# Grouped-query attention: the query norm factor as the exponential's per-row scale, from 16 columns

## The chip, the cores and the metric

The kernel runs on one core of a Trainium2 chip. A core has several engines with queues of their own: TensorE (matmuls; PE in the profile, with its weight loads as PEld), VectorE (DVE), ScalarE (ACT), GpSimd (POOL) and SyncE (SP), which here issues most of the transfers. Each engine takes its instructions in a fixed order. Matmul results go to PSUM, which has eight banks of 128 x 512 fp32 values; everything else lives in SBUF. The metric is the device time of one execution in microseconds, the median of several runs. One execution was also profiled; its rows are what the text quotes.

## The reference

The program is a two-layer encoder over 512 tokens with 1024 features in fp32. Layer 0 mixes neighbourhood attention with a bidirectional state-space scan; layer 1 is grouped-query attention with 16 query heads of 64 features and 4 key/value heads. A gated feed-forward block follows each. The change lies in layer 1:

```python
def odd_mixer(x, mix_norm, w_qkv, q_norm, k_norm, w_out):
    ...
    proj = rms_norm(x, mix_norm) @ w_qkv
    q, k, v = jnp.split(proj, [GQA_Q_WIDTH, GQA_Q_WIDTH + GQA_KV_WIDTH], axis=-1)
    q = rms_norm(q.reshape(Bsz, S, GQA_HEADS, GQA_HEAD_DIM), q_norm)
    k = rms_norm(k.reshape(Bsz, S, GQA_KV_HEADS, GQA_HEAD_DIM), k_norm)
    ...
    q = apply_rope(q, cos, sin)
    k = apply_rope(k, cos, sin)
    return gqa_block_attention(q, k, v) @ w_out
```

`rms_norm` divides a head's 64 features by the root of their mean square (plus 1e-6) and multiplies by a learned gain per feature. So each query of each head has one scalar factor, and the scores of that query, q·k/8, are linear in it. The softmax over the 512 keys follows.

## The kernel before, in words

All activations are kept transposed: features on the 128 partitions, 512 tokens on the free axis. An fp32 product is made of three faster matmuls: each operand is split into a high and a low part (the high part is a rounded copy by ScalarE, the low part a subtraction by VectorE or GpSimd), and low-high, high-low and high-high are summed in PSUM (`mm3`, L165 to L167).

Layer 1 is `odd_mixer`. Its steps, with the names that the rows carry:

- `project` makes the key projection in two banks (`kpa`, `kpb`), and ScalarE and VectorE square it. The sum of squares over the 1024 input features gives two things: `rt`, 4 columns of the input norm factor (tokens on partitions, L1200 to L1205), made by four fp32 matmuls with a slice of `acc` as the stationary operand (`orst`); and `em`, a full 128 x 512 tile of the epsilon term (L1206 to L1209).
- `head_rstd` (L1211) turns squares into a norm factor per head and token, spread over the 32 partitions that belong to the head: one fp32 matmul with the block matrix `bo32` (L1213), a VectorE instruction that adds the epsilon term, then `rsqrt_tile`: logarithm, exponential and square on ScalarE (L214 to L216) and a Newton step of two VectorE instructions (L208, L209). All work on 128 x 512 tiles. It is called once for the keys and once for each of the four query groups.
- `q_blocks(g)` projects one group of four heads in two blocks, each of eight filler steps of three matmuls. Its squares are summed (L1263), and `q_finish` is put off by `OD_AFTER` = 4 steps (`after`, `step`).
- `q_finish(g)` rotates the two halves by the rotary tables (six VectorE instructions, L1171 to L1173), calls `head_rstd`, multiplies both halves by the factor (L1275), splits them (the subtraction is on VectorE for group 0, on GpSimd for the others) and stacks them by 16 transfers into the four `QS` tiles (L1188) that the score matmuls read.
- The sweep (L1410) has 32 steps and three more to drain. Step i issues `scores(i)` for one half of the 512 queries of head i // 2: two tiles of 128 queries by 512 keys. Each takes two matmuls (L1293, L1294) into one of two `s` banks, a row maximum by VectorE (L1296), the exponential with the negative maximum as bias and the row sum as accumulated output by ScalarE (L1298, read out by one more short instruction), a reciprocal by VectorE (L1299) and the scaling by GpSimd (L1300). Step i also transposes the probabilities of step i - 2 (L1309, split at L1312 and L1313) and multiplies those of step i - 3 with the values (L1326, L1327; L1334 to L1337 make the context).
- Between these, `run(fill, n)` takes filler steps from a stream: the projections of groups 1 to 3 (48 steps) and then the blocks of the output projection (two times 32 steps). `OD_FILL` of them come ahead of the sweep and `OD_QUOTA[i]` in step i. An output block waits for the context of its heads with `while ctxb[2 * part + 1] is None: yield`; a step taken while it waits issues nothing.

The order of the instructions on each engine is not quite the program's: in this layer a planner orders them by dependences and its own costs when the program is built, and puts in the waits. In the feed-forward blocks the order of TensorE, VectorE and ScalarE is the written one.

Of the kernel before, what the change touches and what calls it, by code (L numbers as in the profile page):

```python
# [11 lines left out]
AF = mybir.ActivationFunctionType  # L12
ALU = mybir.AluOpType
# [4 lines left out]
P = 128  # L18
S = 512
D = 1024  # L20
KB = D // P
EPS = 1e-6
# [4 lines left out]
HD = 64  # L27
# [14 lines left out]
NSLOT = 12  # L42
NA_QUOTA = (12, 12, 10, 10, 8, 8, 6, 6, 6, 6)
DT_STEP = 96
OD_FILL = 8
OD_AFTER = 4
OD_QUOTA = (5, 5, 4, 2, 2, 2, 2, 2, 2, 8, 2, 2, 2, 2, 0, 0, 3, 2, 5, 0, 3, 6, 1, 0, 2, 1, 1, 3, 1, 1, 6, 2, 2, 2, 2)
LEAD = (15, 12, 14, 8)
SSD_QUOTA = ((10, 9, 10, 0, 12), (10, 8, 10, 5, 12), (11, 8, 10, 0, 15), (10, 8, 10, 1, 12))
NORM_LAG = (12, 14, 10, 8)  # L50
# [27 lines left out]
def encoder_kernel(ctx: ExitStack, tc: tile.TileContext, xt, vec, cst, rope, nab, w_v, w_qk, w_dt, w_ssd,  # L78
                   w_o0, w_t0, w_fa, w_fb, w_kv, w_gv, w_gq, w_o1, out):
    nc = tc.nc  # L80
    V, A, G, T = nc.vector, nc.scalar, nc.gpsimd, nc.tensor
# [13 lines left out]
    def bank(name, tag="p"):  # L95
        if tag in turns:
            turns[tag].append(turns[tag].pop(0))
            tag = turns[tag][-1]
        return pp.tile([P, S], F32, name=name, tag=f"p{tag}", bufs=BANKS[tag])

    def slot(name, dt=F32):
        return sp.tile([P, S], dt, name=name, tag="s")
# [12 lines left out]
    def small(name, cols, bufs=3, parts=P, dt=F32):  # L115
        return sm.tile([parts, cols], dt, name=name, tag=f"sm_{name}", bufs=bufs)
# [9 lines left out]
    def cs(n, w=None):  # L126
        o = COFF[n]
        return cstt[:, o:o + (w or dict(_CST)[n])]
# [42 lines left out]
    def stream(blocks, ahead):  # L171
        ws = []
        for n, (_, matmuls) in enumerate(blocks):
            while len(ws) < min(len(blocks), n + 1 + ahead):
                ws.append(blocks[len(ws)][0]())
            yield from matmuls(ws[n])
# [30 lines left out]
    def newton(r, t, m):  # L207
        V.scalar_tensor_tensor(t, t, -0.5, m, ALU.mult, ALU.mult)  # L208
        V.scalar_tensor_tensor(r, t, 1.5, r, ALU.add, ALU.mult)  # L209

    def rsqrt_tile(m, name):
        r = slot(f"{name}_r")
        t = slot(f"{name}_t")
        A.activation(r, m, AF.Ln)  # L214
        A.activation(r, r, AF.Exp, scale=-0.5)
        A.activation(t, r, AF.Square)  # L216
        newton(r, t, m)
        return r

    def rsqrt_small(m, r, t):  # L220
        A.activation(r, m, AF.Ln)
        A.activation(r, r, AF.Exp, scale=-0.5)
        V.tensor_tensor(t, r, r, ALU.mult)
        newton(r, t, m)
# [926 lines left out]
    def odd_mixer(op):  # L1151
# [15 lines left out]
        def rotate(pa, pb, tabs, name):  # L1167
            outs = []
            for n, (ta, tb, op) in enumerate(((tabs[0], tabs[1], ALU.subtract), (tabs[2], tabs[3], ALU.add))):
                a, b = slot(f"{name}_ra{n}"), slot(f"{name}_rb{n}")  # L1170
                V.tensor_tensor(a, pa, ta, ALU.mult)  # L1171
                V.tensor_tensor(b, pb, tb, ALU.mult)
                V.tensor_tensor(a, a, b, op)  # L1173
                outs.append(a)
            return outs
# [4 lines left out]
        def split(t, name, mk=sslot, eng=V):  # L1180
            hi, lo = mk(f"{name}_sh"), mk(f"{name}_sl")
            A.activation(hi, t, AF.Copy)
            eng.tensor_tensor(lo, t, f(hi), ALU.subtract)
            return hi, lo

        def stack(dst, parts, r):
            for n, src in enumerate(parts):
                nc.sync.dma_start(f(dst)[32 * n:32 * n + 32], f(src)[32 * r:32 * r + 32])  # L1188
# [10 lines left out]
        ra, rb = rotate(pa, pb, ktab, "k")  # L1199
        pst = bank("orst", "c")  # L1200
# [2 lines left out]
        rt, rtm, rtt = small("ort", 4, 1), small("ortm", 4, 1), small("ortt", 4, 1)  # L1203
        V.tensor_scalar(rtm, pst[:, 0:4], 1.0 / D, EPS, ALU.mult, ALU.add)
        rsqrt_small(rtm, rt, rtt)  # L1205
        ss = bank("oss", "c")  # L1206
        T.matmul(ss, ones, acc, start=True, stop=True)
        em = slot("oem")
# [2 lines left out]
        def head_rstd(sq, name):  # L1211
            ps = bank(f"{name}_ss", "s")
            T.matmul(ps, cs("bo32"), sq, start=True, stop=True)  # L1213
            m = slot(f"{name}_m")
            V.scalar_tensor_tensor(m, ps, 1.0 / HD, em, ALU.mult, ALU.add)
            return rsqrt_tile(m, name)

        r = head_rstd(ksq[0], "ok")
# [25 lines left out]
        def step(flush=False):  # L1244
            for item in list(later):
                item[0] -= 1
                if flush or item[0] <= 0:
                    later.remove(item)
                    item[1]()
# [19 lines left out]

        def q_finish(g, banks, sq):  # L1270
            ra, rb = rotate(*banks, qtab, f"q{g}")
            r = head_rstd(sq, f"oq{g}")
            eng = G if g else V
            for t in (ra, rb):
                V.tensor_tensor(t, t, r, ALU.mult)  # L1275
            (ah, al), (bh, bl) = split(ra, f"qa{g}", eng=eng), split(rb, f"qb{g}", eng=eng)
            QS = []
            for j in range(4):
                qs = lane(f"QS{g}_{j}", "qs", 7, F32R)
                stack(qs, (ah, bh, al, bl), j)  # L1280
                QS.append(qs)
            qs_of[g] = QS

        qs_of, pair, probs, trans = {}, {}, {}, {}

        def scores(i):
            h, u = divmod(i, 2)
            g, j = divmod(h, 4)
            QS = qs_of[g]
            pr = []  # L1290
            for t in (2 * u, 2 * u + 1):
                sps = bank(f"os{h}_{t}", "s")
                T.matmul(sps, QS[j][:, t * P:(t + 1) * P], KHL[g][:, 1], start=True, stop=False)  # L1293
                T.matmul(sps, QS[j][:, t * P:(t + 1) * P], KHL[g][:, 0], start=False, stop=True)  # L1294
                mx, sums = small("omx", 1, 6), small("osum", 1, 6)
                V.tensor_reduce(mx, sps, AX.X, ALU.max, negate=True)  # L1296
                p_ = lane(f"op{h}_{t}", "p", PB)
                A.activation(p_, sps, AF.Exp, bias=mx, accum_out=sums)  # L1298
                V.reciprocal(sums, sums)  # L1299
                G.tensor_scalar(p_, p_, sums, 1.0, ALU.mult, ALU.mult)  # L1300
                pr.append(p_)
            probs[i] = pr
# [63 lines left out]
        def run(gen, n=None):  # L1366
            for _ in (gen if n is None else range(n)):
                if n is not None:
                    next(gen, None)
                step()  # L1370
# [13 lines left out]
        for t in range(4):  # L1384
            ps = bank(f"gv{t}", "s")
# [18 lines left out]
        fill = stream(blocks, 2)  # L1404
        run(fill, OD_FILL)
        step(True)
# [3 lines left out]
        for i in range(32 + lag_v):  # L1410
            n = OD_QUOTA[i]
            cuts = (0, (n + 2) // 3, (2 * n + 2) // 3, n)
# [16 lines left out]
    with tc.tile_pool(name="op", bufs=1, reuse_waits="tile") as op:  # L1429
        odd_mixer(op)  # L1430
# [133 lines left out]
```

## Time and profile before

| what | value |
|---|---|
| median of 3 runs | 1268.25 us (1267.84 to 1270.19) |
| profiled execution | 1268.15 us |
| its span, first to last instruction | 1266.3 us |
| granted TensorE clock | 1.000 |
| matmul records | 7574 |
| score tiles: matmul pairs, maxima, exponentials | 64 each |
| query groups through `head_rstd` | 4 |

The profile's page gives for each engine the time in which it was busy; matmuls are pipelined, so a busy TensorE is not always one at its peak. A row of a group of instructions has its line, engine and operation, the tiles out<-in, the shape and count, then the busy time in us, the mean of one in ns, and the idle time of the engine before them with what ended it. A row in order of time has its start and its length in us. A waits row reads: who waited for whom, the total in us, how often, and the longest.

### The profile page before, as it was taken

How to read it: one execution, taken by the hardware profiler on the slowest of the kernel's cores; microseconds unless marked ns; L12 is line 12 of the kernel's file. 1: busy time of each engine (PE TensorE's matmuls, PEld its weight loads, DVE VectorE, ACT ScalarE, POOL GpSimd, SP SyncE). 2: the span in 40 equal slices, each digit the busy share in tenths (PEclk: the TensorE clock that was granted, in tenths of full speed). 3: DMA queues.
4: the chain of work that ended last, by engine and by line, in shares of the span. 5: the costliest groups of instructions: out<-in, count | busy, mean ns of one | idle time of the engine just before them, and what ended most of it. 6: DMA issues, size and time to landing. Idle time of an engine off the chain costs nothing.

```text
span 1266.3 us, 20167 instructions
## 1 busy us (share of the span) xinstructions
PE 1253.5 (99%) x7574; PEld 1098.5 (87%) x7574; DVE 993.4 (78%) x1669; ACT 731.5 (58%) x1384; POOL 119.1 (9%) x161
## 2 busy tenths in 40 slices
PE   9999999999999999999999999999999999999998
PEld 7777788888788999989998888788888999889987
DVE  6788798999779988739954779989779988558732
ACT  6676578778465556515643558787564566326521
POOL 5022110011000000000000014444000000000000
PEclk9999999999999999999999999999999999999999
DMA  6335343546243333323223452320232333323132
GB/s 232 108 108 159 104 150 117 160 142 198 83 149 101 100 109 109 117 84 100 78 80 111 132 126 77 100 51 27 75 121 93 113 107 101 117 83 101 55 119 93
DMA packets 54241, 139.03 MB, mean 110 GB/s; under 512 B 7232, under 2 KB 9664, under 8 KB 54144
## 3 DMA queue, kind: packets, MB, share of 16 engines
q1 hardware_dynamic: 53712, 137.13, 35.1%
q8 instruction: 59, 0.97, 0.3%
q10 hardware_dynamic: 432, 0.63, 0.2%
q14 instruction: 38, 0.31, 0.1%
HBM read 127.11 MB, written 2.23 MB: 102 GB/s over the span
## 4 chain that ended last, share of the span: by engine, by line
PE 94%; DVE 2%; ACT 2%; DMA 1%; issue 0%; DVEq 0%; ACTq 0%
PE fo L165 6%; PE fo L167 6%; PE fo L166 6%; PE fa L167 5%; PE fa L166 5%; PE fa L165 5%; PE fu L1029 3%; PE fg L1029 3%; PE g L165 3%; PE g L166 3%; PE g L167 3%; PE fb L167 3%; PE fb L165 3%; PE fb L166 3%; PE opt L1309 2%; PE vps L286 2%
## 5 line engine op out<-in xcount | busy, mean ns | idle before, releaser
L165 PE MATMUL fo<-hh,wf_l 128*128 128x512 f32 x352 | 137.0, 389 | 0.0
L166 PE MATMUL fo<-hl,wf_h 128*128 128x512 f32 x352 | 137.0, 389 | 0.0
L167 PE MATMUL fo<-hh,wf_h 128*128 128x512 f32 x352 | 136.9, 389 | 0.0
L152 ACT ACTIVATE wf_h<-wf_r 128x1024 fp32r<-128x1024 f32 (+1 forms) x72 | 65.6, 915 | 119.3 <-PE fo L167 67.6
L1002 DVE TENSOR_TENSOR xr<-xr,fo 128x512 f32<-128x512 f32 (+1 forms) x49 | 32.1, 674 | 109.1 <-PE fo L167 109.1
L1300 POOL TENSOR_SCALAR op<-op,osum 128x512 f32<-128x512 f32 x64 | 45.7, 720 | 504.7 <-DMA QS<-qa_sh 433.3
L154 DVE TENSOR_TENSOR wf_l<-wf_r,wf_h 128x1024 fp32r<-128x1024 f32 (+1 forms) x72 | 74.0, 1044 | 11.1 <-ACT wf_h L152 11.1
L166 PEld LDWEIGHTS fo<-hl,wf_h 128*128 128x128 f32 x352 | 66.1, 188 | 13.8
L167 PEld LDWEIGHTS fo<-hh,wf_h 128*128 128x128 f32 x352 | 66.1, 188 | 13.8
L165 PEld LDWEIGHTS fo<-hh,wf_l 128*128 128x128 f32 x352 | 66.1, 188 | 13.5
L165 PE MATMUL g<-n_xh,w_l 128*128 128x512 f32 x192 | 76.9, 401 | 0.8 <-ACT grp L546 0.8
L166 PE MATMUL g<-n_xl,w_h 128*128 128x512 f32 x192 | 75.3, 392 | 0.5 <-DVE n_xl L189 0.5
L167 PE MATMUL g<-n_xh,w_h 128*128 128x512 f32 x192 | 75.3, 392 | 0.0
L926 ACT ACTIVATE sl<-sb 128x256 f32<-128x256 f32 x36 | 15.1, 421 | 96.0 <-DVE sb L925 96.0
L1298 ACT ACTIVATE op<-os,omx 128x512 f32<-128x512 f32 x64 | 43.8, 687 | 17.3 <-DVE omx L1296 16.7
L807 ACT ACTIVATE sa<-fa 128x256 f32<-128x256 f32 x72 | 27.0, 375 | 37.9 <-PE fa L167 37.9
L1313 DVE TENSOR_TENSOR opt<-opt,opt 128x512 fp32r<-128x512 f32 x64 | 43.4, 683 | 4.8 <-ACT opt L1312 4.2
L1312 ACT ACTIVATE opt<-opt 128x512 fp32r<-128x512 f32 x64 | 38.2, 597 | 14.7 <-PE opt L1309 14.2
L1296 DVE TENSOR_REDUCE omx<-os 128x1 f32<-128x512 f32 x64 | 42.3, 680 | 5.0 <-PE os L1294 4.7
L810 DVE TENSOR_TENSOR gl<-gr,gh 128x1024 fp32r<-128x1024 f32 x36 | 43.9, 1218 | 0.0
L165 PEld LDWEIGHTS g<-n_xh,w_l 128*128 128x128 f32 x192 | 36.1, 188 | 8.4 <-ACT grp L546 1.2
L807 ACT ACTIVATE gh<-gr 128x1024 fp32r<-128x1024 f32 x36 | 37.7, 1049 | 9.4 <-PE fo L167 9.4
(2745 smaller groups left out, 4314.8 us busy)
## 6 DMA issues: line engine op xcount, KB each, us to landing
ur<-in_w_fa SPq DMA_DIRECT2D x36, 512.0 KB, 3.6
gr<-in_w_fa SPq DMA_DIRECT2D x36, 512.0 KB, 3.6
w_r<-in_w_ssd SPq DMA_DIRECT2D x24, 512.0 KB, 3.6
wf_r<-in_w_fb SPq DMA_DIRECT2D x32, 320.0 KB, 3.0
wf_r<-in_w_fa SPq DMA_DIRECT2D x16, 512.0 KB, 3.7
wf_r<-in_w_fb SPq DMA_DIRECT2D x16, 512.0 KB, 3.5
nb<-in_nab SPq DMA_DIRECT2D x16, 256.0 KB, 3.1
ec<-ecumd SPq DMA_DIRECT2D x32, 128.0 KB, 2.9
```

The source lines that it names most:

```text
L152: A.activation(hi[:, 0:cols], raw, AF.Copy)
L154: (eng or V).tensor_tensor(lo[:, 0:cols], raw, f(hi)[:, 0:cols], ALU.subtract)
L165: T.matmul(ps, wl[:, a], xh[:, b], start=first, stop=False, skip_group_check=skip)
L166: T.matmul(ps, wh[:, a], xl[:, b], start=False, stop=False, skip_group_check=skip)
L167: T.matmul(ps, wh[:, a], xh[:, b], start=False, stop=last, skip_group_check=skip)
L807: A.activation(dst, src, AF.Copy, scale=scale)
L810: V.tensor_tensor(lo, t, f(hi), ALU.subtract)
L1029: T.matmul(ps, (wl if p == 0 else wh)[:, k * P:k * P + P], xl if p == 1 else xh, start=m == 0, stop=m == 23)
L1296: V.tensor_reduce(mx, sps, AX.X, ALU.max, negate=True)
L1298: A.activation(p_, sps, AF.Exp, bias=mx, accum_out=sums)
L1300: G.tensor_scalar(p_, p_, sums, 1.0, ALU.mult, ALU.mult)
L1313: V.tensor_tensor(hl[:, S:2 * S], pt, f(hl[:, 0:S]), ALU.subtract)
```

## The change

The factor of a query no longer goes into the query. `q_finish` leaves the rotated query as it is and makes the factor as 16 columns, with the tokens on the partitions: for each of the four blocks of 128 tokens one matmul with that slice of the squares as stationary operand and four columns of `bo32` (one per head of the group) as the moving one. The epsilon term comes from `emc`, four columns made beside `rt`, and the root from `rsqrt_small`, which does the same steps on the small tile. The score tile in PSUM is then without its factor; `scores` multiplies the negative row maximum by the factor (128 x 1, VectorE) and gives the factor as the exponential's scale per row. The keys are treated as before. `OD_FILL` and four entries of `OD_QUOTA` change as well.

```diff
-OD_FILL = 8
+OD_FILL = 9
 OD_AFTER = 4
-OD_QUOTA = (5, 5, 4, 2, 2, 2, 2, 2, 2, 8, 2, 2, 2, 2, 0, 0, 3, 2, 5, 0, 3, 6, 1, 0, 2, 1, 1, 3, 1, 1, 6, 2, 2, 2, 2)
+OD_QUOTA = (5, 5, 1, 2, 2, 2, 2, 2, 2, 8, 2, 2, 2, 3, 0, 0, 3, 8, 5, 0, 3, 6, 1, 0, 2, 1, 1, 3, 1, 1, 6, 0, 2, 2, 2)
...
         rsqrt_small(rtm, rt, rtt)
+        emc = small("oemc", 4, 1)
+        V.tensor_scalar(emc, pst[:, 0:4], EPS / D, EPS * EPS, ALU.mult, ALU.add)
...
             ra, rb = rotate(*banks, qtab, f"q{g}")
-            r = head_rstd(sq, f"oq{g}")
+            ps = bank(f"oq{g}_ss", "s")
+            for t in range(4):
+                T.matmul(ps[:, 4 * t:4 * t + 4], sq[:, t * P:(t + 1) * P], cs("bo32")[:, 0:P:32], start=True, stop=True)
+            m, r, tt = (small(f"oq{n}", 16, 2) for n in "mrt")
+            V.scalar_tensor_tensor(m.rearrange("p (t j) -> p t j", t=4), ps[:, 0:16].rearrange("p (t j) -> p t j", t=4),
+                                   1.0 / HD, emc.unsqueeze(2).to_broadcast([P, 4, 4]), ALU.mult, ALU.add)
+            rsqrt_small(m, r, tt)
+            rows[g] = r
             eng = G if g else V
-            for t in (ra, rb):
-                V.tensor_tensor(t, t, r, ALU.mult)
...
                 V.tensor_reduce(mx, sps, AX.X, ALU.max, negate=True)
+                row = rows[g][:, 4 * t + j:4 * t + j + 1]
+                V.tensor_tensor(mx, mx, row, ALU.mult)
                 p_ = lane(f"op{h}_{t}", "p", PB)
-                A.activation(p_, sps, AF.Exp, bias=mx, accum_out=sums)
+                A.activation(p_, sps, AF.Exp, bias=mx, scale=row, accum_out=sums)
```

More of the change, by code (lines that the diff above doesn't have):

```diff
@@ L1282, in q_finish @@
             qs_of[g] = QS
-        qs_of, pair, probs, trans = {}, {}, {}, {}
+        qs_of, rows, pair, probs, trans = {}, {}, {}, {}, {}
         def scores(i):
```

## The prediction

> **What bounds the kernel now.** I read the page first, then the busy time by stretches over the second half, then the waits of TensorE in the stretches where it is not full, then rows in order of time for the price of single instructions.
>
> ```profile
> span 1266.3 us, 20167 instructions
> PE 1253.5 (99%) x7574; PEld 1098.5 (87%) x7574; DVE 993.4 (78%) x1669; ACT 731.5 (58%) x1384; POOL 119.1 (9%) x161
> ```
>
> The profiled execution took 1268.15 us: the span of 1266.3 and 1.85 around it. All sums below start there; the median of the runs, 1268.25, is 0.1 higher. TensorE is busy for 99% of the span, so nothing that VectorE or ScalarE save is worth anything by itself. It counts only where TensorE waits for them, or where TensorE's own work changes. The query norm lies in the grouped-query layer; its sweep over 32 steps of two score tiles (16 heads by two halves) runs from 747.8 to 886.5 us. Stretches of it, with the columns PE, weight loads, DVE, ACT, POOL, granted clock, DMA share and GB/s:
>
> ```profile
> 750.00:800.00 50.00, 49.81 (x281) 42.01 (x280) 45.44 (x88) 36.43 (x77) 18.22 (x23) 1.00 0.42 114
> 800.00:840.00 40.00, 37.71 (x216) 29.78 (x214) 36.57 (x74) 32.01 (x70) 21.56 (x25) 1.00 0.25 60
> 840.00:880.00 40.00, 40.00 (x257) 34.85 (x255) 36.32 (x76) 32.67 (x73) 17.56 (x24) 1.00 0.11 34
> 880.00:905.00 25.00, 24.98 (x143) 20.66 (x142) 17.88 (x31) 13.97 (x28) 4.72 (x6) 1.00 0.15 44
> L1293 PE MATMUL os<-K,QS x64: 387/398/682, 747.8 to 886.5; 128*128 128x512 f32 x64
> ```
>
> TensorE shows 0.19 us of idle time in the first stretch, 2.29 in the second, none in the third. VectorE stands at 91% in all three: here it is nearly a second bound. The waits, TensorE's from 800 to 840 us (five rows), from 750 to 800 (the sixth), and last the weight loads' waits for the exponential from 700 to 910:
>
> ```profile
> PE opt L1309 <- DVE opt L1313: 0.7, 1, 0.7
> PE oq_ss L1213 <- ACT op L1298: 0.5, 1, 0.5
> PE o L165 <- ACT cx_sh L1182: 0.4, 1, 0.4
> PE os L1293 <- ACT op L1298: 0.3, 1, 0.3
> PE oc L1326 <- DVE ocx L1335: 0.2, 1, 0.2
> PE os L1293 <- ACT op L1298: 0.2, 1, 0.2
> PEld os L1293 <- ACT op L1298: 4.6, 12, 0.7
> ```
>
> These 2.3 us are what the sweep loses in plain sight. Some more is hidden: a score matmul's weight load waits 12 times for an exponential to free one of the two score banks, 4.6 us in all, of which 0.5 comes out as idle TensorE.
>
> **TensorE's share of the change.** Per query group, one 512-column fp32 matmul goes, and four come whose stationary operand is a 128x128 slice of the squares and whose moving operand has four columns. Their form stands in the trace at L1202, with one column:
>
> ```profile
> 715.03 0.95 PE L1202 MATMUL orst<-cstt,o_acc 128*128 128x1 f32 x8
> 717.56 1.02 PE L1213 MATMUL ok_ss<-oksq,cstt 128*128 128x512 f32 x2
> ```
>
> Each fp32 matmul leaves two records. Four small ones take 0.95 us, the wide one 1.02. So 4 x (0.95 - 1.02) = -0.3 us; sixteen columns are not a sixteenth of the price. Bounds: 0 to -0.3.
>
> **VectorE and ScalarE in the norm.** Removed per group are five wide VectorE instructions (L1215, L208, L209, twice L1275) and three wide ScalarE ones (L214 to L216). A queue of them runs at this pace:
>
> ```profile
> 820.01 0.68 DVE L1171 TENSOR_TENSOR q_ra<-q,qt_tab 128x512 f32<-128x512 f32 x1
> 820.62 0.68 DVE L1172 TENSOR_TENSOR q_rb<-q,qt_tab 128x512 f32<-128x512 f32 x1
> 821.21 0.68 DVE L1215 SCALAR_TENSOR_TENSOR oq_m<-oq_ss,oem 128x512 f32<-128x512 f32 x1
> 821.81 0.68 DVE L1173 TENSOR_TENSOR q_ra<-q_ra,q_rb 128x512 f32<-128x512 f32 x1
> 821.95 0.62 ACT L214 ACTIVATE oq_r<-oq_m 128x512 f32<-128x512 f32 x1
> 822.60 0.63 ACT L215 ACTIVATE oq_r<-oq_r 128x512 f32<-128x512 f32 x1
> 823.27 0.63 ACT L216 ACTIVATE oq_t<-oq_r 128x512 f32<-128x512 f32 x1
> ```
>
> From start to start that is 0.60 us on VectorE and 0.66 on ScalarE: 3.0 and 2.0 us less per group. Group 0 is finished before the sweep, so within the sweep VectorE loses 9.0 and ScalarE 6.0. What replaces them are four small VectorE and two small ScalarE instructions per group, and 64 multiplications of 128x1, one per score tile, between the row maximum and the exponential. The price of a small instruction depends on its neighbours:
>
> ```profile
> 844.77 0.16 DVE L1299 RECIPROCAL osum<-osum 128x1 f32<-128x1 f32 x1
> 844.85 0.67 DVE L1356 TENSOR_TENSOR xr<-xr,o 128x512 f32<-128x512 f32 x1
> 720.69 0.16 DVE L223 TENSOR_TENSOR ortt<-ort 128x4 f32<-128x4 f32 x1 [1.01 <-ACT ort L222]
> 720.77 0.69 DVE L1381 TENSOR_TENSOR wgvl<-wgv_r,wgvh 128x512 fp32r<-128x512 f32 x1
> 721.37 0.15 DVE L208 SCALAR_TENSOR_TENSOR ortt<-ortt,ortm 128x4 f32<-128x4 f32 x1
> 721.45 0.68 DVE L1209 TENSOR_SCALAR oem<-oss 128x512 f32<-128x512 f32 x1
> 722.04 0.15 DVE L209 SCALAR_TENSOR_TENSOR ort<-ortt,ort 128x4 f32<-128x4 f32 x1
> 30.57 0.16 DVE L223 TENSOR_TENSOR rtt<-rt 128x4 f32<-128x4 f32 x1
> 30.76 0.16 DVE L208 SCALAR_TENSOR_TENSOR rtt<-rtt,rtm 128x4 f32<-128x4 f32 x1
> ```
>
> With another wide instruction behind it, a small one moves the queue on by 0.08 us (844.77 to 844.85), though it lasts 0.16. Directly behind the instruction that it depends on it costs 0.20 (30.57 to 30.76). Bounds of one multiplication are thus 0.08 and 0.20. I take 0.08, because in the same layer (720.69 to 722.04) the planner put a wide instruction between each pair of a dependent chain. The 64 then cost 5.1 us (12.8 at the other end), the three groups' small ones 12 x 0.08 = 1.0 (2.4). VectorE's balance over the sweep is -9.0 + 5.1 + 1.0 = -2.9 us, or +6.2 at the other end.
>
> The duration alone speaks against the change: 0.16 us for one column against 0.68 for 512. [...]
>
> The exponential gets a second per-row operand. The trace has one activation with both from PSUM, against today's exponential:
>
> ```profile
> L530 ACT ACTIVATE grp<-g,vect 128x512 f32<-128x512 f32 x16 | 12.4, 775 | 19.3 <-PE g L167 19.3
> L1298 ACT ACTIVATE op<-os,omx 128x512 f32<-128x512 f32 x64 | 43.8, 687 | 17.3 <-DVE omx L1296 16.7
> L222 ACT ACTIVATE ort<-ort 128x4 f32<-128x4 f32 x1 | 0.2, 206 | 0.0
> ```
>
> That is 88 ns more, 5.6 us over 64. With the six small ones at 0.2 each (the last row), 1.2 us, ScalarE's balance in the sweep is -6.0 + 5.6 + 1.2 = +0.8 us: nothing at 73 to 82% busy. The new small term emc (L1206 of the new file) is one more 0.15 us beside 0.68 us instructions, hidden under gv matmuls: nothing.
>
> **What of it reaches TensorE.** First, the burst. After the third group's projection VectorE runs six rotations, then the five norm instructions, between 816 and 829 us, and score tiles queue behind them. The rotations stay, and so do the waits for ocx, cx_sh and the bank of oq_ss (1.1 us of the five rows). The waits that come after (0.7 for the transposed probabilities, 0.3 for the exponential) go with 3.0 us of norm work taken out ahead of them; about half as much again is hidden in slower matmul starts: -1.5. The first two bursts show 0.2 and something hidden: -0.3. Second, the price: every tile's bank is held longer by 0.08 + 0.09 = 0.17 us. On 12 waits this is 2.0 us if all comes out and 0.2 at the share that comes out now (0.5 of 4.6); I take 0.2, since the score matmuls have other matmuls ahead of them.
>
> Third, the filler. Counting the steps that the quotas allow, after stage 2 the new kernel has done 20 where the old one had 22, after stage 12 46 against 48, after stage 13 49 against 50, and from stage 16 both stand at 52. There the next step needs the context of heads 6 and 7, which stage 18 delivers; steps asked for until then yield without a matmul. So the quota of 8 in stage 17 moves nothing, and both reach 53 in stage 18 and leave 28 for the end. The third query group's finish comes one stage (about 4.3 us) later, behind stage 15:
>
> ```profile
> 840.68 0.59 SPq L1188 DMA_DIRECT2D QS<-qb_sl  x1
> 855.08 0.48 PE L1293 MATMUL os<-K,QS 128*128 128x512 f32 x1
> L165 PE MATMUL g<-n_xh,w_l 128*128 128x512 f32 x192 | 76.9, 401 | 0.8 <-ACT grp L546 0.8
> ```
>
> Its last stacking transfer is issued 14.4 us before the first scores of that group, so the delay is covered, and the shorter chain gives some of it back. No transfer is added; the sixteen of a group only come ready sooner. Two filler steps of three matmuls fewer in the early stages cost nothing while TensorE's idle time there is 0.2 us; without cover it is at most 2 x 3 x 0.40 = 2.4.
>
> The sum: -0.3 - 1.5 - 0.3 + 0.2 = -1.9 us, 1268.15 - 1.9 = 1266.3 us. Against the median this is 0.16% less, and about 0.2% (2.5 us) is what a measurement of this kernel tells from no change.
>
> **The rivals.** One: all that waits is relieved. The visible 2.5 us of 750 to 905 go, and half of the 4.6 of the weight loads with them: 1268.15 - 2.5 - 2.3 = 1263.4. For it: VectorE, at 91%, is the one that is late in the burst. Against: three of the five visible waits stand ahead of the removed work. Chance 0.23.
>
> Two, slower: the multiplication stands directly behind its maximum and VectorE becomes the bound after the bursts.
>
> ```profile
> 800.00:840.00 40.00, 11.86 (x18) 1.00 0.25 60
> 840.00:880.00 40.00, 13.31 (x21) 1.00 0.11 34
> ```
>
> These are the row maxima in two stretches. In the second nothing is removed, and 21 multiplications at 0.20 take 4.2 us where VectorE has 3.68 free; in the first 18 x 0.20 = 3.6 eat the 3.0 that the burst saves. With VectorE's free time there mostly forced by its inputs, some 3 of the 4.2 us come out: 1268.15 + 3 = 1271.2. It decides from 3.68 / 21 = 0.175 us per tile on. For it is the pair at 30.57; against, the chain at 720.69. [...] Chance 0.19.
>
> Three, it does nothing: TensorE's work is even, and a new order puts as many waits elsewhere as it removes: 1268.2. For it is that 99% leave little. Chance 0.18.
>
> **How the numbers follow.** The forecast has 0.40, with its own range 1264.8 to 1267.5; about a third of it lies below 1265.7 and counts as faster. Faster is then 0.23 + 0.14 = 0.37, slower 0.19, and the rest, 0.44, is the same. The range reaches from below rival one's 1263.4 to rival two's 1271.2: 1262.4 to 1271.2.
>
> **What would show it.** Right: the small matmuls at about 0.95 us per group; the exponential near 775 ns; TensorE's idle time from 800 to 840 us down from 2.3 to about 1.2, with ocx and cx_sh still in the list; small multiplications with a wide instruction ahead of them; nothing moved before 715 us, and the last feed-forward layer shifted as a whole. Wrong: the weight loads' waits for the exponential well above 4.6 us, or VectorE over 95% from 840 to 880 us; or a saving over 4 us, which the waits named here could not hold without the hidden ones.

## The result, and the profile after

The changed kernel takes 1278.28 us (median of 4 runs, 1277.93 to 1280.85) against 1268.14 us of the kernel before beside it: ratio 1.0086, 95% interval 1.0074 to 1.0098. That is 10.1 us more, where 1.9 us less was forecast, and above the end of the range (1271.2). The profiled execution took 1278.18 us, its span is 1276.2.

The page of the kernel after, first lines:

```profile
span 1276.2 us, 20222 instructions
PE 1262.8 (99%) x7598; PEld 1098.9 (86%) x7598; DVE 996.5 (78%) x1730; ACT 730.0 (57%) x1380; POOL 121.0 (9%) x161
```

TensorE is still "99% busy", and 9.3 us longer so, in a span that is 9.9 us longer: busy time doesn't show the loss. The stretches of the sweep, columns as in the prediction (PE, weight loads, DVE, ACT, POOL, clock, DMA share, GB/s):

```profile
750.00:800.00 50.00, 49.43 (x278) 40.88 (x277) 42.92 (x99) 33.89 (x71) 19.32 (x23) 1.00 0.38 100
800.00:840.00 40.00, 37.37 (x218) 29.49 (x216) 36.85 (x87) 30.20 (x65) 18.51 (x22) 1.00 0.34 91
840.00:880.00 40.00, 39.09 (x230) 31.77 (x229) 36.05 (x87) 31.28 (x67) 16.51 (x22) 1.00 0.13 37
880.00:905.00 25.00, 24.92 (x153) 20.76 (x152) 22.46 (x50) 18.70 (x39) 10.67 (x13) 1.00 0.12 30
```

The counts hint at it: from 840 to 880 us TensorE now runs 230 matmuls where it ran 257. They are no measure, because the windows hold other work: the sweep starts at 749.5 us instead of 747.8, and in another order. Waits of the weight loads and of TensorE from 740 us on, after:

```profile
PEld os L1300 <- ACT op L1307: 9.4, 29, 0.7
PEld oc L1335 <- DVE opt L1322: 4.9, 11, 0.9
...
PE os L1300 <- ACT op L1307: 1.4, 5, 0.4
```

The score matmuls' weight loads wait for an exponential 29 times instead of 12 and twice as long in all (9.4 against 4.6 us). The two new operations themselves, by groups:

```profile
L1307 ACT ACTIVATE op<-os,omx,oqr 128x512 f32<-128x512 f32 x64 | 49.4, 776 | 12.9 <-DVE omx L1305 12.6
L1305 DVE TENSOR_TENSOR omx<-omx,oqr 128x1 f32<-128x1 f32 x64 | 12.8, 204 | 0.1
```

Where the time went, by the starts of the same matmuls in both traces: the first projection starts 0.65 us later (87.02 against 86.37; over all the traces of this study it lies between 85.0 and 87.0); from there to the key projection of layer 1 it takes 619.2 us instead of 617.8 (+1.4), although nothing in this stretch was changed; layer 1, from there to the start of the last feed-forward block, takes 220.5 instead of 213.1 (+7.4); the last block adds 0.4. So there are two losses, one of them outside the edited code.

### The profile page after: what moved, and what is told of

It is laid out like the page before. It is cut to its first block, busy times and chain, and to the rows that moved or that the text cites. A ratio compares the mean times of both kernels' runs of the same rounds, so it can differ in the third digit from the quotient of the medians.

```text
span 1276.2 us, 20222 instructions
## 1 busy us (share of the span) xinstructions
PE 1262.8 (99%) x7598; PEld 1098.9 (86%) x7598; DVE 996.5 (78%) x1730; ACT 730.0 (57%) x1380; POOL 121.0 (9%) x161
## 4 chain that ended last, share of the span: by engine, by line
PE 92%; DVE 4%; ACT 2%; issue 1%; DMA 0%; POOL 0%; DVEq 0%; ACTq 0%; POOLq 0%
PE fo L166 6%; PE fo L167 6%; PE fo L165 6%; PE fa L167 5%; PE fa L165 5%; PE fa L166 5%; PE fu L1029 3%; PE fg L1029 3%; PE g L166 3%; PE g L165 3%; PE g L167 3%; PE fb L165 3%; PE fb L167 3%; PE fb L166 3%; PE vps L286 2%; PE opt L1318 1%
## 5 line engine op out<-in xcount | busy, mean ns | idle before, releaser
L1307 ACT ACTIVATE op<-os,omx,oqr 128x512 f32<-128x512 f32 x64 | 49.4, 776 | 12.9 <-DVE omx L1305 12.6
```

The source lines that it names most:

```text
L1307: A.activation(p_, sps, AF.Exp, bias=mx, scale=row, accum_out=sums)
```

## Experiments

All times are medians. "Above before" is the difference to the kernel before in the same batch, whose median lay between 1267.46 and 1268.28 us. The way of a tile is the time from the start of its maximum to the start of its exponential.

**Parts of the change, left as the planner orders them.** First the multiply is taken off the way to the exponential, left out, or kept without the scale:

```diff
# e1 (e2 has the second pair alone, without the multiply)
-V.tensor_tensor(mx, mx, row, ALU.mult)
+V.tensor_tensor(small("ojk", 1, 6), mx, row, ALU.mult)
-A.activation(p_, sps, AF.Exp, bias=mx, scale=row, accum_out=sums)
+A.activation(p_, sps, AF.Exp, bias=mx, scale=one1, accum_out=sums)
# e3
-V.tensor_tensor(mx, mx, row, ALU.mult)
+V.tensor_tensor(mx, mx, one1, ALU.mult)
-A.activation(p_, sps, AF.Exp, bias=mx, scale=row, accum_out=sums)
+A.activation(p_, sps, AF.Exp, bias=mx, accum_out=sums)
```

> The multiplication of the row maximum is still issued for each of the 64 score tiles, but writes a tile that nothing reads; the exponential takes the plain maximum as bias and a column of ones as scale (the query norm factor is left out of the scores). Chain theory (the multiplication stands one wide VectorE instruction behind its maximum, so that each score bank is held about 0.7 us longer): 1269 to 1272 us, the weight loads' waits for the exponential fall from 9.4 to below 6 us. Occupancy theory (VectorE is full, 64 more instructions are too many): stays at 1277 to 1279. Scale theory (the exponential's second operand, 88 ns a tile): stays at 1277 to 1279. Filler theory: stays.

> The multiplication is not issued at all; the exponential takes the plain maximum as bias and a column of ones as scale (the query norm factor is left out of the scores). Chain theory: like the run with the multiplication off the chain, within 1.5 us (1269 to 1272). Occupancy theory: 1268 to 1271, and clearly below the run that issues it off the chain. Scale theory and filler theory: 1276 to 1279.

> The multiplication stays in the chain, with a column of ones in place of the factor, and the exponential has no scale operand (the query norm factor is left out). Chain theory and occupancy theory: 1275 to 1278, at most 2 us less than the changed kernel. Scale theory: 1269 to 1272; the exponential back at about 687 ns in either case.

Measured: e1, off the way, 1279.69 us (ratio 1.0091, 1.0076 to 1.0106); e2, without the multiply, 1273.97 (1.0046, 1.0032 to 1.0061); e3, without the scale, 1280.82 (1.0098, 1.0083 to 1.0113). Taking the multiply out of the way gains nothing, taking it out altogether gains 4.3 us, and the scale is not the cause (in e3 too the norm factor stays out of the scores). Without the multiply 5.8 us of the loss are still there.

All three times lie outside the ranges of every theory, e1's by 0.7 us, and e1 speaks against the chain theory: its way is 1.02 us in the mean, where the kernel after has 2.01, and yet it is no faster. Its weight loads wait 11.7 us for the exponential, not less than 6. Layer 1 by itself takes 219.8 us in e1, 216.4 in e2 and 223.3 in e3, against 220.5 in the kernel after. (The column of ones in e1 to e3 is one more tile, which moves the addresses behind it; the matmuls compared under Addresses below take 392 and 394 to 396 ns in these three, as in the kernel after.)

The change with the old filler numbers (`OD_FILL = 8`, the old `OD_QUOTA`):

> The changed kernel with the filler numbers of the kernel before (8 ahead of the sweep, the old list). Filler theory (the two filler steps that are moved, and the third group's finish one stage later, cost the time): 1269 to 1272. Chain, occupancy and scale theory: 1275 to 1281, on either side of the changed kernel.

Measured 1280.6 us (1.0097, 1.008 to 1.0114), 2.3 us more than the kernel after. The intervals of the two overlap, so a gain by the new numbers is not certain; the loss they are not.

**Addresses.** The change's small tiles (416 bytes per partition) lie ahead of the layers' pools and move all tiles in these by 416 bytes. The kernel has an unused tile in the same place, so its length undoes the shift, or makes it alone:

```diff
# e5, in the kernel after        # e6, in the kernel before
-SHIFT = 136                     -SHIFT = 136
+SHIFT = 32                      +SHIFT = 240
```

> The changed kernel with its unused padding tile 416 bytes per partition shorter, so that every tile of the layers' pools lies at the address that it has in the kernel before (the change's small tiles had moved them all by 416 bytes). Address theory: the 1.9 us that the changed kernel loses outside the grouped-query layer, where its instructions and their order are those of before, come back (key projection again at about 704.2 us), and matmuls there go back from 392 to 389 ns; 1274 to 1276.5 us, or less if matmuls in the layer gain too. Occupancy theory alone (64 more VectorE instructions): 1277 to 1279, the key projection stays at 706 us.

> The kernel before with its padding tile 416 bytes per partition longer and nothing else changed. Address theory: 1270 to 1272 us, with the key projection at about 706 us. Occupancy theory alone: 1267 to 1269.

Measured: after at the old addresses 1275.12 us (1.006, 1.0043 to 1.0077); before at the new ones 1271.31 (1.0028, 1.0017 to 1.0039). Not one instruction differs between before and e6. Groups of the high-high matmuls of two products, from 100 to 690 us, of the kernel before, after, and after at the old addresses:

```profile
L167 PE MATMUL fo<-hh,wf_h 128*128 128x512 f32 x155 | 60.3, 389 | 0.0
L167 PE MATMUL oA<-so_xh,wo_h 128*128 128x512 f32 x32 | 12.5, 390 | 0.0
```

```profile
L167 PE MATMUL fo<-hh,wf_h 128*128 128x512 f32 x152 | 59.6, 392 | 0.0
L167 PE MATMUL oA<-so_xh,wo_h 128*128 128x512 f32 x32 | 12.7, 396 | 0.0
```

```profile
L167 PE MATMUL fo<-hh,wf_h 128*128 128x512 f32 x156 | 60.7, 389 | 0.0
L167 PE MATMUL oA<-so_xh,wo_h 128*128 128x512 f32 x32 | 12.5, 390 | 0.0
```

The same matmul takes 3 to 6 ns longer at the other addresses. In e6's trace this makes 1.9 us from the first projection to layer 1, 0.7 in layer 1 and 0.4 after it. Of the 10.1 us it is 2.5 (by e5, 10.1 - 7.7) to 3.9 (by e6). By the sizes of the kernel's tiles, these operands and the weights all start 96 bytes past a multiple of 128 before; the shift puts those in the layers' pools on a multiple of 128. Whether that is what matters is open: only one shift was tried.

**One part added to the kernel before.** All of these stand at the old addresses.

```diff
# e7: behind the maximum
+                V.tensor_tensor(mx, mx, ones[:, 0:1], ALU.mult)
# e8
-                A.activation(p_, sps, AF.Exp, bias=mx, accum_out=sums)
+                A.activation(p_, sps, AF.Exp, bias=mx, scale=ones[:, 0:1], accum_out=sums)
```

> The kernel before, wide query norm and all, with one multiplication of each row maximum by a column of ones, at unchanged addresses. Occupancy theory: 1271 to 1275 us (64 instructions of 0.08 to 0.2 us are 5 to 13 us more on a VectorE that is 91% busy). If the multiplication only costs where the small norm has changed the order: 1268 to 1270.

> The kernel before with a column of ones as the exponential's scale operand, at unchanged addresses. Scale theory: 1270 to 1273 us (88 ns more on each of 64 exponentials, each holding a score bank longer). Occupancy theory of VectorE: 1267.5 to 1269.5; the exponential near 775 ns either way.

Measured: with the multiply 1278.65 us (1.0089, 1.0074 to 1.0104), 11.2 above before; with the scale 1268.63 (1.0008, 0.9999 to 1.0018). e7 lies above both of its theories, e8 in the range of the second. So 64 multiplies of one column cost 11 us when added, yet only 4.3 when removed. Prices that don't add up ask for a third thing that changes along.

**Other forms of the multiply, and the norm alone**, all in the kernel after at the old addresses:

```diff
# e9
-V.tensor_tensor(mx, mx, row, ALU.mult)
+V.tensor_scalar(mx, mx, row, 1.0, ALU.mult, ALU.mult)
# e10: once for both tiles of a step
+V.tensor_tensor(mx, mx, rows[g][:, 8 * u + j:8 * u + j + 5:4], ALU.mult)
# e11: no multiply, and
-A.activation(p_, sps, AF.Exp, bias=mx, scale=row, accum_out=sums)
+A.activation(p_, sps, AF.Exp, bias=mx, accum_out=sums)
# e12: instead of maximum and multiply (row holds the negative factor; the exponential's scale is -1)
+V.tensor_tensor_reduce(sps, sps, zero1.to_broadcast([P, S]), row, 3e38, ALU.add, ALU.min, mx)
```

> The changed kernel with the addresses of before (1275.12 us as measured), the multiply written so that its factor is a per-partition scalar operand and only the maximum is a tensor operand; all else as it was. In the changed kernel 12 or 13 of the 64 multiplies last 0.2 to 1.1 us, each of these over a running GpSimd operation and ending with it, while the reciprocal, which reads one tensor, never does. Theory one (two reads from SBUF wait for GpSimd): the long ones go, their excess is some 0.05 us x 64 = 3 us by the mean, so 1270 to 1272.5 us, and no multiply lasts over 0.2 us. Theory two (any further operation in the row costs its slot, whoever it waits for): 1274 to 1276 us.

> The changed kernel with the addresses of before (1275.12 us), one multiply of 128x2 for the two tiles of a sweep step instead of two of 128x1: 32 multiplies, the same values. Both maxima now stand ahead of the multiply, so that the first tile's exponential starts about one wide operation (0.7 us) later. Theory one (each multiply has a price of its own, 11.2 us by 64 as the kernel before with the multiply showed): half of it goes, 1269 to 1270.5 us. Theory two (what costs is the way from the scores to the exponential): 1275 to 1280 us.

> The changed kernel with the addresses of before (1275.12 us), without the multiply and without the scale of the exponential: only the small norm in place of the wide one is left (the norm factor is left out of the scores). Theory one (prices add up as they were measured when added to the kernel before: 11.2 us for the multiply, 1.2 us for the scale): 1275.1 - 12.4 = 1262.7 us, 5 us below before. Theory two (prices as measured when taken from the changed kernel: 4.3 us for the multiply): 1275.1 - 4.3 - 1.2 = 1269.6 us, so the small norm by itself gains nothing and the planner's new order loses something.

> The changed kernel with the addresses of before (1275.12 us); the maximum and the multiply are one VectorE operation, which scales the scores in their bank by the negative norm factor and keeps the minimum; the exponential then takes the scaled scores with a fixed scale of -1. The same values, 64 operations fewer in the sweep, four small ones more in the norm. Theory one (each further operation costs): 1275.1 less 11.2, and a few us more if the fused operation lasts longer than the maximum (0.1 us longer is 64 x 0.1 = 6.4 us of VectorE): 1263 to 1270 us, at the best below both kernels. Theory two (a wide operation that reads its second operand from SBUF and writes the bank back waits for GpSimd or holds the bank): 1275 us or more.

Measured: e9 1276.93 us (1.0072, 1.0057 to 1.0087); e10 1274.72 (1.0051, 1.0035 to 1.0068); e11 1269.82 (1.0017, 1.0008 to 1.0026); e12 1273.21 (1.0044, 1.0029 to 1.0059). e9 and e10 miss their theory two by 0.9 and 0.3 us, e12 lies between its two theories.

e9 was made for rows like these, of the kernel after in order of time (start, length):

```profile
826.49 1.29 POOL L1183 TENSOR_TENSOR cx_sl<-ocx,cx_sh 128x512 fp32r<-128x512 f32 x1
826.96 0.83 DVE L1305 TENSOR_TENSOR omx<-omx,oqr 128x1 f32<-128x1 f32 x1
827.72 0.68 DVE L1322 TENSOR_TENSOR opt<-opt,opt 128x512 fp32r<-128x512 f32 x1
```

A multiply of one column lasts 0.83 us and ends with GpSimd's subtraction. With the factor as a per-partition scalar that is gone. The line of e9's multiplies (shortest, median, longest in ns):

```profile
L1305 DVE TENSOR_SCALAR omx<-omx,oqr x64: 194/205/215, 748.7 to 898.3; 128x1 f32<-128x1 f32 x64
```

None is longer than 215 ns, and the time is not better. But the mean is 205 ns where it was 204, so VectorE spends the same time in the multiplies: e9 shows that it does not matter whether a few are long or all a little longer, not that their time costs nothing. Halving the number (e10) changed little too; there the way grows to 2.49 us. The norm alone (e11) is 1.9 us slower than before, so theory two of that run holds: the small norm by itself brings nothing. The fused form (e12) is no way out: its operation lasts 749 ns where the maximum takes 682, and an accumulator read of 139 ns follows each of the 64, which is again a small operation between the scores and the exponential:

```profile
L1307 DVE CUSTOM_DVE_ANT_0 os<-os,zero,oqm 128x512 f32<-128x512 f32 x64 | 46.7, 749 | 7.6 <-PE os L1304 7.5
...
L1307 DVE DVE_READ_ACCUMULATOR2_ANT omx<- 128x1 f32 x64 | 8.9, 139 | 0.0
```

**The order held.** What changes along is the order. The planner orders all of layer 1 anew when one instruction is added. By the order lists used below, 462 of layer 1's 1178 TensorE instructions stand elsewhere with the multiply added to the kernel before (e7). (The 803 of 1600 in the expectation of f1 does not come out of these lists.) How far the others go can be seen by laying the first 1600 TensorE records from the key projection on beside those of before: 38 find no partner with the scale alone (e8), 326 with the multiply (e7), 363 with the small norm alone (e11) and 528 with the whole change at the old addresses (e5). So order and work were held separately. In the next kernels a list gives each engine's order in layer 1, and edges between neighbours that carry no wait force it:

```diff
+ORDER = {"PE": ..., "DVE": ..., "Activation": ..., "Pool": ..., "SP": ...}
...
+        for a, b in zip(rows, rows[1:]):
+            tc.add_manual_dep(b, a.name, mybir.DependencyInfo(mybir.DependencyClass.NoSync, mybir.DependencyReason.DATA),
+                              reason="order")
...
         odd_mixer(op)
+        fix_order(nc, tc, start)
# f3, f4 also
-            m, r, tt = (small(f"oq{n}", 16, 2) for n in "mrt")
+            m, r, tt = (small(f"oq{n}", 16, 4 if n == "r" else 1) for n in "mrt")
```

> The kernel before with the 64 multiplies of the maximum by a column of ones (as in the run of before with the multiply, 1278.65 us), but with the instructions of layer 1 held on every engine in the order that the kernel before has; each multiply stands one VectorE operation behind its maximum. Same addresses, same work as that run. Theory one (the planner's new order costs, 803 of 1600 places on TensorE differ from before): 1268 to 1271 us, the rest being VectorE's time for the multiplies. Theory two (the multiplies themselves cost 0.17 us each): 1277 to 1280 us.

> The kernel before, without any multiply, held in the order that the planner made for the kernel with the 64 multiplies. Nothing is added, only places are changed. Theory one (order): 1274 to 1279 us. Theory two (the multiplies themselves): 1268 us.

> The whole change (small norm, multiply, scale) at the addresses of before, with the old quotas and with layer 1 held in the order of before: the small operations of the norm stand in the places of the wide ones that they replace, each multiply one VectorE operation behind its maximum. The factor has four buffers instead of two, since in the order of before group 3's factor is made (821.2 us) before group 1's last exponential has ended (825.3 us). Theory one (order and addresses cost, the change by itself does what the prediction's sum says): 1264 to 1269 us. Theory two (the multiplies and the scale themselves): 1275 to 1280 us.

> As the run with the whole change in the order of before, without the multiply and the scale (the factor is left out of the scores): only the small norm is left, in the places of the wide one. Theory one (order): the norm alone, relieved as the prediction's rival one has it, 1263 to 1267 us, below the 1269.8 us that it took in the planner's own order. Theory two (a norm made of small operations is worth nothing): 1268 to 1270 us.

Measured: f1 (e7's work in the order of before) 1292.03 us (1.019, 1.0177 to 1.0204), 24.2 above before; f2 (before's work in e7's order) 1274.56 (1.0051, 1.0039 to 1.0064), 6.7 above; f3 (the whole change in the order of before) 1294.78 (1.0215, 1.0201 to 1.0229), 26.9 above; f4 (the norm alone in it) 1268.02 (1.0001, 0.9992 to 1.001).

f2 and f4 came out as one of their theories says (order for f2, a norm worth nothing for f4); f1 and f3 missed both. The new order does cost, 6.7 us with nothing else in it, but it is no accident of the planner: in the old order the multiply costs over twice as much as in the order that was made for it. The waits of f1 from 747 to 907 us, and below of f1's weight loads:

```profile
PE os L1339 <- ACT op L1346: 10.3, 22, 1.2
PE oq_ss L1259 <- ACT op L1346: 3.3, 3, 1.5
...
```

```profile
ACT op L1346 <- DVE omx L1343: 41.1, 35, 2.9
PEld os L1339 <- ACT op L1346: 23.0, 34, 1.4
```

That is one chain: the exponential waits for the multiply (41 us, where it waited 16.7 us for the maximum), the score bank stays taken, the next score matmul waits for the bank. The last two runs separate this delay from VectorE's time. In f1 each multiply stands one VectorE operation behind its maximum (two for 16 of the 64); in g1 directly behind it (`GAP = 0` instead of 1); in g2 it stands where f1 has it, but writes a tile that nothing reads, and the exponential takes the maximum.

> As the kernel before with the 64 multiplies in the order of before (1292.03 us, 24 above before), but each multiply stands directly behind its maximum instead of one VectorE operation further. Theory one (the way from the scores to the exponential: with an operation of 0.6 us in between, a tile's bias and bank come about 0.75 us later, directly behind some 0.2): the loss shrinks with the delay, 24 x 0.2 / 0.75 = 6 us, 1272 to 1277 us. Theory two (VectorE's time): a small operation directly behind the one that it depends on takes more of the engine than one with another operation between, so 1290 us or more.

> As the kernel before with the 64 multiplies in the order of before (1292.03 us), each at the same place, one VectorE operation behind its maximum, but the product goes to a tile that nothing reads, and the exponential takes the maximum itself. VectorE does the same work; nothing waits for the multiply. Theory one (the way from the scores to the exponential): 1268 to 1271 us. Theory two (VectorE's time for the multiplies): 1287 to 1292 us.

Measured: g1 1279.0 us (1.0084, 1.007 to 1.0097), 10.7 above before; g2 1273.54 (1.0041, 1.0027 to 1.0055), 5.3 above. Both lie above the range of theory one, by 2.0 and 2.5 us, and far below theory two: the way is the larger part, but VectorE's time is not free. TensorE's waits for the score banks, g1 and then g2:

```profile
PE os L1339 <- ACT op L1346: 2.9, 6, 1.0
PE oq_ss L1259 <- ACT op L1346: 1.4, 3, 0.6
```

```profile
PE os L1339 <- ACT op L1346: 1.1, 4, 0.5
```

The means of the ways of the 64 tiles, from the rows in order of time, beside the loss:

| kernel | order | maximum to exponential, us | above before, us |
|---|---|---|---|
| before | its own | 1.00 | 0 |
| g2: multiply off the way | before's | 0.96 | 5.3 |
| g1: multiply directly behind | before's | 1.15 | 10.7 |
| f1: one operation between | before's | 1.69 | 24.2 |
| f2: no multiply | e7's | 1.97 | 6.7 |
| e7: multiply | e7's | 2.12 | 11.2 |
| f3: the whole change | before's | 1.74 | 26.9 |
| f4: small norm alone | before's | 1.06 | 0.1 |
| after, at before's addresses (e5) | its own | 2.01 | 7.7 |
| after | its own | 2.01 | 10.1 |
| e1: after, multiply off the way | its own | 1.02 | 11.6 |
| e11: small norm alone | its own | 0.92 | 1.9 |

f1 and g2 are the clean pair. Order, addresses and VectorE's work are the same; they differ in whether the exponential waits for the multiply. That alone costs 24.2 - 5.3 = 18.9 us, for exponentials that start 1.69 - 0.96 = 0.73 us later: 26 us for each microsecond of way, which over 64 tiles is 0.4 us of time for 1 us of delay, in the mean. f3, the whole change in that order, fits it. g1 can't be divided as cleanly. Directly behind its maximum a multiply starts 0.71 us after the maximum's start, where in g2 VectorE's next operation starts after 0.62 us; over 64 tiles that is about 6 us more of VectorE's time, and g1's 5.4 us above g2 may be this or the delay.

From one order to another the way does not tell the loss. The planner's order for e7 has a way of 1.97 us even without a multiply (f2) and costs 6.7 us; with the multiply e7 loses only 4.5 us more. e1 has the short way, in yet another order, and loses 11.6 us, no less than the kernel after with the long one (10.1). What the planner's orders pay with was not measured apart.

## Why the prediction was wrong, by its own steps

The sum was -0.3 - 1.5 - 0.3 + 0.2. The two reliefs, -1.5 and -0.3, came out as nothing (f4: 0.1 us above before). The multiply's +0.2 is the term furthest off: with the scale it costs 5.8 us in the planner's orders (e5 against e11). And two costs had no term at all, the addresses (2.5 to 3.9 us) and the new order of layer 1 (6.7 us in f2, for the kernel before).

**"I take 0.08, because in the same layer the planner put a wide instruction between each pair of a dependent chain."** For VectorE's queue this holds in the middle and not in the sum. In the kernel after the median multiply moves the queue on by 0.08 us, but 30 of the 64 by more, and together (each from its start to the next start, at most to its end) they take 9.4 us instead of 5.1. The sum let VectorE's time cost nothing; g2, which adds the multiplies to the kernel before and lets nothing wait for them, loses 5.3 us. The planner did put a wide operation between the two, for 56 of 64 tiles. What failed is the next step, **"every tile's bank is held longer by 0.08 + 0.09 = 0.17 us"**. The wide operation that makes the multiply cheap for VectorE stands on the way from the scores to the exponential. A tile of the kernel after in order of time, VectorE's rows and then ScalarE's:

```profile
853.95 0.68 DVE L1303 TENSOR_REDUCE omx<-os 128x1 f32<-128x512 f32 x1
854.54 1.22 DVE L154 TENSOR_TENSOR wo_l<-wo_r,wo_h 128x1024 fp32r<-128x1024 f32 x1
855.68 0.15 DVE L1308 RECIPROCAL osum<-osum 128x1 f32<-128x1 f32 x1
855.75 0.14 DVE L1305 TENSOR_TENSOR omx<-omx,oqr 128x1 f32<-128x1 f32 x1
```

```profile
855.77 0.60 ACT L1321 ACTIVATE opt<-opt 128x512 fp32r<-128x512 f32 x1 [0.52 <-PE opt L1318]
856.27 0.77 ACT L1307 ACTIVATE op<-os,omx,oqr 128x512 f32<-128x512 f32 x1
```

Two tiles of the kernel before, with a weight split on VectorE at the same place:

```profile
846.65 1.27 DVE L1296 TENSOR_REDUCE omx<-os 128x1 f32<-128x512 f32 x2
847.85 1.21 DVE L154 TENSOR_TENSOR wo_l<-wo_r,wo_h 128x1024 fp32r<-128x1024 f32 x1
```

```profile
847.42 0.69 ACT L1298 ACTIVATE op<-os,omx 128x512 f32<-128x512 f32 x1
...
848.10 0.68 ACT L1298 ACTIVATE op<-os,omx 128x512 f32<-128x512 f32 x1
```

Before, the first exponential has started and the second runs while the split is on VectorE; neither waits for it. After, the maximum is done at 854.6, the split and the multiply come first, then a copy on ScalarE, and the exponential starts at 856.27, 2.3 us after the start of its maximum. In the mean the way is 2.01 us instead of 1.00, and from the start of a tile's first score matmul to the end of its exponential it is 4.13 us instead of 3.41: a bank is held 0.72 us longer, not 0.17. The two ends of the bound, 0.08 and 0.20, were taken as a cheap and a dear case of one cost. In the order of before they were two costs that exclude each other: little VectorE time and a long way, or a short way and more VectorE time.

That the longer hold costs time is shown in the order of before (f1 against g2). In the changed kernel's own order it is not shown: in e1, whose order is another again, the banks are held 3.69 us, and the time is no better. There the cause of the multiply's 5.8 us stays open between the way, VectorE's time and the new order.

**"0.2 at the share that comes out now (0.5 of 4.6)".** The share was taken from the 12 waits of a kernel that had slack. By f1 and g2 a delay of 0.17 us would cost 26 x 0.17 = 4.4 us in the order of before, not 0.2. The sign that was named, weight loads that wait well above 4.6 us, did come (9.4 us), but these waits do not measure the loss: e11 has 9.0 us of them and is 1.9 us slower than before.

**"The waits that come after go with 3.0 us of norm work taken out ahead of them: -1.5", and -0.3 for the first bursts.** f4 shows no such relief. Its stretch from 800 to 840 us and TensorE's waits there:

```profile
800.00:840.00 40.00, 37.70 (x224) 30.34 (x223) 33.40 (x72) 30.68 (x71) 21.34 (x24) 1.00 0.25 61
```

```profile
PE opt L1362 <- DVE opt L1366: 0.7, 1, 0.7
PE oq_ss L1322 <- ACT op L1351: 0.5, 1, 0.5
PE o L211 <- ACT cx_sh L1228: 0.4, 1, 0.4
PE os L1346 <- ACT op L1351: 0.3, 1, 0.3
```

VectorE lost 3.2 us of work there, as forecast (33.40 against 36.57), and TensorE's waits are the same four to a tenth: only the 0.2 for ocx is gone. So the wide norm was not what those waits were late for. VectorE at 91% had looked like a second bound, but freed time on it was worth nothing, while 64 operations more cost 5.3 us (g2). That also takes away rival one, which expected more of the same relief.

**"Nothing moved before 715 us."** Wrong, and not weighed at all: the key projection starts at 706.24 us instead of 704.15 (0.65 of it ahead of the first projection, 1.4 in the unchanged stretch behind it), and e5, with the whole change at the old addresses, has it at 703.44. The addresses are 2.5 to 3.9 us of the 10.1.

**The smaller terms.** The exponential was forecast at 775 ns and takes 776; that it costs nothing by itself holds within e8's interval, whose middle is 1 us. The four small matmuls of a group take 1.06 us (first group at 733.74) instead of 0.95, no gain over the wide one's 1.02. The new filler numbers may have gained 2.3 us (e4, intervals overlapping). The last group's finish comes 10.3 us later (831.5 instead of 821.2 us), not 4.3, and its first scores 10 us later (865.1 instead of 855.1). The last stacking transfer is issued at 842.05, so the finish is still covered. In the order of before its factor would be made before group 1's last exponential had read the factor that lies in the same buffer, which is why f3 and f4 have four.

**Rival two** had the right side and the wrong place. It priced a multiply directly behind its maximum by VectorE's time, 3 us from 0.175 us per tile on. g1 has such a multiply, in the old order and with the wide norm kept, and loses 10.7 us. The dearer pair that the rival feared is real there: the multiply starts 0.71 us after the start of its maximum, where in g2 the next operation starts after 0.62. In the changed kernel it is rare, 2 of 64 tiles, and VectorE is busy for 36.05 of the 40 us from 840 to 880, not for over 95%. The 0.15 us that an undisturbed multiply lasts come to 9.6 us over the 64; VectorE's queue pays 9.4, where the sum had 5.1, though by 0.08 us in the median and by more for 30 of them.

The account of the 10.1 us, by differences: addresses 2.5; the small norm in the planner's order 1.9 (e11); multiply and scale in the planner's order 7.7 - 1.9 = 5.8. The last two of these differences also hold a new order. How the last term divides into order, delay and VectorE's time was not shown for the changed kernel's own order. No run of the change or of a part of it was faster than the kernel before; with the multiply and the scale for nothing, in the best order at hand, it is a tie (f4).

## What to carry to other kernels

Price an operation that goes into a dependent chain by the latency it adds to the chain, with whatever the order puts between it and its input, and multiply by how often the chain holds a scarce buffer; in f1 engine time was 5.3 of 24.2 us. Do not count work taken from an engine that is 90% busy as a gain until a wait of the bounding engine is shown to end with that work; here it was worth nothing (f4). Where a planner orders the code, test an edit once in the old order and once with the old work in the new order, and keep the addresses of everything else fixed; otherwise the parts' prices don't add up.

## What the hardware showed beyond expectation

- The 416 bytes by which e6 moves the SBUF tiles of the layers are worth 0.3% of this kernel: 389 against 392 ns and 390 against 396 ns per matmul, 3.9 us (ratio 1.0028, 1.0017 to 1.0039) with not one instruction changed. Only one shift was tried by itself.
- The one-column multiply of the kernel after, with two SBUF operands, lasts 0.15 us in the median and up to 1.03 us beside a GpSimd operation: each of the 11 above 0.2 us starts while one runs and ends within 0.03 us of its end. One that starts 0.04 us behind the start of a GpSimd operation (at 841.56 us) lasts 0.15 us all the same. With one tensor operand and a per-partition scalar all 64 take 194 to 215 ns (e9).
- In g2 the granted clock fell after a short gap. Three stretches of 3.4 us (clock in the third column from the end):

```profile
830.22:833.62 3.40, 1.59 (x8) 0.93 (x8) 3.13 (x6) 3.03 (x8) 2.80 (x3) 1.00 0.08 19
833.63:837.03 3.40, 3.40 (x15) 3.21 (x15) 2.48 (x8) 1.56 (x4) 1.68 (x3) 0.50 0.42 96
837.04:840.44 3.40, 3.19 (x22) 2.68 (x21) 2.84 (x8) 2.33 (x5) 1.25 (x3) 1.00 0.47 109
```

After 1.8 us of idle TensorE between 830.2 and 833.6 the granted clock falls to one half for 3.4 us, which is 1.7 us of clock. Three of g2's five executions have a mean clock of 0.998 and took 1273.5 to 1274.1 us; the two at 1.000 took 1272.6 and 1273.2. So the clock is some 0.8 us of g2's 5.3, by so few executions only roughly. In e12 it fell likewise: TensorE is busy for 2.02 us from 816 to 820 us, and from 820 to 824 the clock is 0.59 in the mean. In f1 it stayed at 1.00 from 804 to 812 us, with 2.82 busy us in the first four.
